# A hybrid decoder trunk on one core: next x transposed as float32r from copied pieces, two chunks behind its gate

## The chip, the cores and the metric

The kernel runs on one core of a Trainium2 chip. The metric is the device time in microseconds, the median of 3 runs. Before the change it is 1412.37 us (1411.79 to 1412.73).

The engines have these names in the profile: PE (matmul; PEld is its weight load), DVE (vector), ACT (scalar), POOL and SP (which here mostly issue DMAs).

## What is computed

Two decoder layers over 512 tokens of 1024 numbers. Each layer mixes tokens, adds the result to its input and normalizes it, runs a squared-ReLU MLP with a normalization behind it, and ends with a gate:

```python
for i in range(DEPTH):
    mix = ssd_mixer(x, ...) if i % 2 == 0 else hgrn2_mixer(x, ...)
    h = layer_norm(DEEPNORM_ALPHA * x + mix, ln_g[i, 0], ln_b[i, 0])
    h = layer_norm(DEEPNORM_ALPHA * h + sq_relu_mlp(h, mlp_w1[i], mlp_w2[i]), ln_g[i, 1], ln_b[i, 1])
    x = h + jax.nn.sigmoid(h @ ple_w_gate[i]) * (p[i] @ ple_w_proj[i])
```

All inputs and outputs are float32. The change lies where the last line is done for the first layer (the first gate) and its result, the next x, is prepared for the second layer's token mixer (HGRN2).

## The kernel before, in words

**Numbers and tiles.** A float32 matrix product is made from three products of float32r operands: each operand is split into hi, a float32r copy made by ACT (L113), and lo, the rest, made by DVE (L116). mm3 (L119 to L122) issues hi*hi, hi*lo and lo*hi into one PSUM bank. The 512 tokens are four chunks of 128 (index c), the 1024 columns two halves of 512 (index h). acc holds the running x with the tokens on the partitions; the products need x with its columns on the partitions, so x is transposed on PE.

**Places.** b8 is a pool of nine places of 8 KB a partition (L52). The split h (h_s, four places) and the split next x (x_n, L616, four places) live there during the first gate; the ninth is free there and is taken later by s3 of values4 (put, L679). PSUM has eight banks: four for pj, one for pt, two for py, one for pm (L57 to L60).

**The first gate** is the end of mlp_and_gate (L616 to L670). For each half h and each chunk c there are 24 matmuls into a bank pg (L658 to L660), then a sigmoid on ACT (L663), a multiplication with the projected p (L664, DVE) and the addition into acc (L666, DVE). The finished 128x512 piece of next x is then turned: turn(h, c) (L620 to L630) transposes it from acc with four PE transposes of 128x128 in float32 against the identity (ident, a part of the constants) into the one bank pt (L625), and three operations read pt one after another: ACT casts it to x_n.hi (L628), ACT copies it to rows (L629), DVE makes x_n.lo (L630). The turn of a chunk isn't issued at once but appended to a list, late, and issued behind the next chunk's gate (L667 to L669). So when the gate ends, one turn is left over.

**values4** (L672 to L729) is the first work of the second layer: the value and gate projections of its first heads, as seven products of 24 matmuls. PE's order is the program's order there (tc.manual_schedule, L1008). Behind the first product stand the left-over turns; then come the others:

```python
        product(part(0, 0), [unit(v) for v in w[0][0]], x, True, first(0, 0))
        for f in late:
            f()
        product(part(0, 1), [unit(v) for v in w[1][0]], z, True, more(0, 0))
```

The first product reads columns of half 0 and tokens of chunks 0 and 1; the second half 1 of the same tokens; the third s3, a difference of two blocks of rows, made at L708 and split at L681 and L682. The later products need the other blocks of rows and the weight sums that DVE makes from weights loaded by POOL (weight_sums, L322).

**Order.** Outside the parts with a written order the framework's scheduler orders each engine's instructions by priority and readiness and sets the waits; each engine then works through its list in order.

Of the kernel before, what the change touches and what calls it, by code (L numbers as in the profile page):

```python
# [9 lines left out]
F32R = mybir.dt.float32r  # L10
# [5 lines left out]
P = 128  # L16
T = 512
# [27 lines left out]
def trunk(ctx: ExitStack, tc, a):  # L45
    nc = tc.nc
    pool = lambda name, bufs, **kw: ctx.enter_context(tc.tile_pool(name=name, bufs=bufs, **kw))
    cpool = pool("consts", 1)
# [3 lines left out]
    b8 = pool("b8", 9)  # L52
# [11 lines left out]
    def nm(s):  # L64
        uid[0] += 1
        return f"{s}_{uid[0]}"

    def mk(p, shape, tag, dt=F32, **kw):
        return p.tile(list(shape), dt, tag=tag, name=nm(tag), **kw)

    def f32(t):
        return t.bitcast(F32)
# [16 lines left out]
    def tmp(tag, shape, dt=F32):  # L89
        return mk(phase[0], shape, tag, dt, bufs=phase[2].get(tag, 1))  # L90

    def bank(p, tag):
        return mk(p, [P, T], tag)
# [8 lines left out]
    def unit(src, lead=LEAD, after=None):  # L102
        n = src.shape[1]
        with tc.high_priority(offset=lead):
            raw = mk(raws, [P, 1024], "raw")
            nc.sync.dma_start(raw[:, :n], src)
        return split(raw[:, :n], lead, after)
# [29 lines left out]
    def project(src, xs, ps, m=P, tok=slice(0, T)):  # L137

        hi, lo = src
        for k in range(8):  # L140
            c = slice(k * m, (k + 1) * m)
            mm3(ps[:m, tok], hi[:, c], lo[:, c], xs.h(k, tok), xs.l(k, tok), k == 0, k == 7)
# [4 lines left out]
    acc = mk(accp, [P, NCH, D], "acc")  # L147
# [32 lines left out]
    ident, triu, eps = cols["ident"], cols["triu"], cols["eps"]  # L180
    convw = cols["convw"].rearrange("p (i k) -> p i k", k=4)
    convb, dskip, snw, hlb, hnw = (cols[n] for n in ("convb", "dskip", "snw", "hlb", "hnw"))
    dtc = cols["dtc"]
    ones = tmp("cm", [P, P])
    nc.gpsimd.memset(ones, 1.0)
    one = mk(cpool, [P, 1], "one")
    nc.gpsimd.memset(one, 1.0)
    ones_s = mk(cpool, [P, 64], "ones_s")
    nc.gpsimd.memset(ones_s, 1.0 / 512)


# [93 lines left out]
    def norm(i, keep=None):  # L285

        gb = ln_params(i)
        h_s = Split(8)
        sums = mk(sm, [P, NCH, 2], "lnsum") if i else None

        def chunk(c):
            with tc.high_priority(offset=LEAD if c == 3 and i % 2 == 0 else 0 if c > 1 and i == 1 else SOON):
                layer_norm(i, c, gb, sums)

        return h_s, chunk, lambda c: transpose_split(acc[:, c, :], h_s, c, c == 3 and i % 2 == 0, keep), sums
# [262 lines left out]
    def mlp_and_gate(layer, h_s, last):  # L558

        w1, w2 = a[f"w1_{layer}"], a[f"w2_{layer}"]  # L560
        blocks = {}
        low = turned_last[0]

        def hidden(g):
            names = ("a11", "a12", "a22", "s1", "s2", "s3", "s4")
            blocks[g] = {
                n: tmp("blk", [P, 2, 4, 256], F32R) if n in ("s3", "s4") else mk(b8, [P, 2, 4, 256], "b8", F32R)
                for n in names
            }
            for p in range(2):  # L570
                tiles = [4 * (2 * g + r) + 2 * p + i for r in range(2) for i in range(2)]
                us = []
                if g == p == 0:
                    for m in tiles[:3]:
                        us.append((unit(w1[m]), bank(psj, "pj")))
                        project(us[-1][0], h_s, us[-1][1], tok=slice(0, 256))
                zs = []
                for r in range(2):
                    z = mk(w4, [P, 2, T], "ab"[r])
                    for i in range(2):  # L580
                        if 2 * r + i < len(us):
                            u, ps = us[2 * r + i]
                            project(u, h_s, ps, tok=slice(256, 512))
                        else:
                            ps = bank(psj, "pj")
                            project(unit(w1[tiles[2 * r + i]], after=low if g == 0 and r == 0 else None), h_s, ps)
                        nc.scalar.activation(z[:, i], ps, AF.Relu)
                        if i == 1:
                            nc.scalar.activation(z, z, AF.Square)
                            zs.append(z)  # L590
                            if r == 1:
                                half_blocks(blocks[g], *zs, p)
                        yield

        for g, period in enumerate(PERIODS):
            if g < 4:
                tiles = hidden(g)
            if g > 0:
                if g == 4:
                    kept = tmp("blk", [P, 2, 4, 256]) if last else None  # L600
                    h_s, after, turned, sums = norm(2 * layer + 1, kept)
                    p_s = (mk(w4, [P, 2, T], "a", F32R), mk(w4, [P, 2, T], "b", F32R))
                    praw = mk(raws, [P, 1024], "raw")
                    nc.sync.dma_start(praw, a[f"pT_{layer}"].rearrange("p k t -> p (k t)"))
                    praw = praw.rearrange("p (k t) -> p k t", k=2)
                    nc.scalar.copy(p_s[0], praw)
                    nc.vector.tensor_sub(p_s[1], praw, f32(p_s[0]))
                w = [[[w2[8 * g - 8 + 4 * i + 2 * j + u] for u in range(2)] for j in range(2)] for i in range(2)]
                products = block_product(w, blocks.pop(g - 1), SUMS[g - 1], g == 1, *((after, turned(0), sums) if g == 4 else ()), low=low if g == 1 else None)
            for op in period:  # L610
                next(tiles if op == "T" else products)

        if last:
            return last_gate(a[f"wp_{layer}"], a[f"wg_{layer}"], h_s, p_s, kept, turned)

        x_n = Split(8)  # L616
        rows = [tmp("blk", [P, 2, 4, 256]) for _ in range(2)]
        late = []

        def turn(h, c):  # L620

            sl = slice(c * P, (c + 1) * P)
            pt = bank(pst, "pt")
            for j in range(4):
                nc.tensor.transpose(pt[:, j * P : (j + 1) * P], acc[:, c, h * 512 + j * P : h * 512 + (j + 1) * P], ident)  # L625
            v = pt.rearrange("p (j t) -> p j t", j=4)
            hh = x_n.hi[h][:, :, sl]
            nc.scalar.copy(hh, v)  # L628
            nc.scalar.copy(rows[c // 2][:, h, :, c % 2 * P : (c % 2 + 1) * P], v)  # L629
            nc.vector.tensor_sub(x_n.lo[h][:, :, sl], v, f32(hh))  # L630

        pps = {}

        def proj(c, pu):

            ps = pps[c] = bank(*((psj, "pj") if c > 1 and pps else (psy, "py%d" % (c % 2))))
            sl = slice(c * P, (c + 1) * P)
            for k in range(2):
                ks = slice(k * 512, (k + 1) * 512)
                mm3(ps, p_s[0][:, k, sl], p_s[1][:, k, sl], pu[0][:, ks], pu[1][:, ks], k == 0, k == 1)  # L640

        for h in range(2):
            pu = unit(a[f"wp_{layer}"][h])
            gu = [unit(a[f"wg_{layer}"][4 * h + j]) for j in range(4)]
            for c in range(NCH):
                sl = slice(c * P, (c + 1) * P)
                if h == c == 0:
                    turns = turned(1)
                    for i in range(NCH):
                        proj(i, pu)  # L650
                        if i in (1, 2):
                            next(turns)
                if h == 1:
                    proj(c, pu)
                turns = turned(c + 2) if h == 0 and c < 2 else None
                pg = bank(psj, "pj")
                sg = tmp("sg", [P, T])
                for k in range(8):  # L658
                    ks = slice((k % 2) * 512, (k % 2 + 1) * 512)
                    mm3(pg, h_s.h(k, sl), h_s.l(k, sl), gu[k // 2][0][:, ks], gu[k // 2][1][:, ks], k == 0, k == 7)  # L660
                    if turns and k in (2, 5):
                        next(turns)
                nc.scalar.activation(sg, pg, AF.Sigmoid)  # L663
                nc.vector.tensor_mul(sg, pps.pop(c), sg)  # L664
                d = acc[:, c, h * 512 : (h + 1) * 512]
                nc.vector.tensor_add(d, sg, d)  # L666
                while late:  # L667
                    late.pop(0)()
                late.append(lambda h=h, c=c: turn(h, c))  # L669
        return x_n, rows, late  # L670

    def values4(xs, rows, late):  # L672
# [333 lines left out]
    x_s, rows, late = mlp_and_gate(0, h_s, False)  # L1006
# [457 lines left out]
```

## Time and profile before

| What | Value |
|---|---|
| median of 3 runs | 1412.37 us |
| span of the profiled execution | 1409.6 us |
| PE busy | 1404.3 us, 100% of the span, 8001 matmuls |
| DVE busy | 1069.1 us, 76% |
| ACT busy | 763.6 us, 54% |
| POOL busy | 45.8 us, 3% |
| first gate to its last matmul | about 705 to 760 us from the span's start |
| values4 on PE | from about 760 us |

The profiled execution's own time is its span of 1409.6 us with what lies around it; no separate time is given for it, and 2.8 us lie between the span and the median of the runs. Lines of the timeline give the start in us from the span's beginning, the length in us, engine, line, operation, and out<-in by the program's names; b is a place of b8 (or of a pool for weights and results), pt the transposes' bank, r a loaded weight block, blk a block of rows. In [...] stands the idle time of the engine before the instruction, and what ended it. The recorded lengths of PE's instructions overlap, since they are pipelined: what an instruction costs is read from the distance of the starts, or from the chain of waits.

### The profile page before, as it was taken

The page shows a single profiled execution, that of the slowest core. Times are in us where ns is not written, and L with a number is a line of the kernel's source. Part 1 is how long each engine was busy: PE and PEld are TensorE (multiplying, and loading weights), DVE is VectorE, ACT ScalarE, POOL GpSimd, SP SyncE. Part 2 cuts the span into 40 slices and gives each one's busy share as a digit, 9 for nine tenths or more (in the row PEclk, how much of TensorE's full clock was granted, in tenths as well). Part 3 has the DMA queues.
Part 4 walks back from the last instruction along what each step waited for, and adds up shares of the span by engine and source line. Part 5 has one row for each costly group of instructions (what it writes and reads, how often), then busy time and mean ns, then how long its engine had stood idle before and what let it go on. Part 6 is the DMA issues. An engine that isn't in the chain of part 4 may idle for free.

```text
span 1409.6 us, 20400 instructions
## 1 busy us (share of the span) xinstructions
PE 1404.3 (100%) x8001; PEld 1168.1 (83%) x8001; DVE 1069.1 (76%) x1778; ACT 763.6 (54%) x1156; POOL 45.8 (3%) x92
## 2 busy tenths in 40 slices
PE   9999999999999999999999999999999999999998
PEld 7888888888988888888888888888898888888887
DVE  7989688698977668677986577678785867667795
ACT  7766465573354444545555547655555454544573
POOL 0000000001000000000000000000100000000100
PEclk9999999999999999999999999999999999999999
DMA  8433333234433444345621421222443444444731
GB/s 313 135 117 120 106 120 110 85 100 156 141 113 127 157 131 152 129 142 178 209 90 49 134 91 61 76 87 96 150 135 105 147 137 148 144 137 159 202 106 60
DMA packets 50399, 181.69 MB, mean 129 GB/s; under 512 B 5632, under 2 KB 6400, under 8 KB 50176
## 3 DMA queue, kind: packets, MB, share of 16 engines
q1 hardware_dynamic: 38784, 138.45, 29.6%
q0 software_dynamic: 11520, 41.95, 9.2%
q8 instruction: 63, 1.03, 0.3%
q14 instruction: 32, 0.26, 0.1%
HBM read 177.16 MB, written 2.16 MB: 127 GB/s over the span
## 4 chain that ended last, share of the span: by engine, by line
PE 99%; DMA 0%; DVE 0%; issue 0%; DVEq 0%
PE pj L120 25%; PE pj L121 25%; PE pj L122 25%; PE py L120 5%; PE py L122 5%; PE py L121 5%; PE py L906 1%; PE pt L238 1%; PE py L1175 1%; PE pm L923 1%; PE pm L871 1%; PE py L1301 1%; PE pt L859 0%; PE py L1303 0%; PE py L1240 0%; PE py L832 0%
## 5 line engine op out<-in xcount | busy, mean ns | idle before, releaser
L113 ACT CAST whi<-raw 128x1024 fp32r<-128x1024 f32 x218 | 228.8, 1050 | 333.2 <-PE pj L121 243.6
L120 PE MATMUL pj<-b,whi 128*128 128x512 f32 (+1 forms) x990 | 378.6, 383 | 0.0
L122 PE MATMUL pj<-b,wlo 128*128 128x512 f32 (+1 forms) x990 | 376.8, 381 | 0.0
L121 PE MATMUL pj<-b,whi 128*128 128x512 f32 (+1 forms) x990 | 376.6, 381 | 0.0
L116 DVE TENSOR_TENSOR wlo<-raw,whi 128x1024 fp32r<-128x1024 f32 x218 | 265.4, 1221 | 129.4 <-ACT whi L113 128.2
L121 PEld LDWEIGHTS pj<-b,whi 128*128 128x128 f32 x990 | 186.4, 188 | 34.6 <-issue 0.9
L122 PEld LDWEIGHTS pj<-b,wlo 128*128 128x128 f32 x990 | 186.3, 188 | 34.5
L120 PEld LDWEIGHTS pj<-b,whi 128*128 128x128 f32 x990 | 186.1, 188 | 34.0
L122 PE MATMUL pj<-whi,b 128*128 128x512 f32 x520 | 204.1, 392 | 0.0
L120 PE MATMUL pj<-whi,b 128*128 128x512 f32 x508 | 202.1, 398 | 0.0
L121 PE MATMUL pj<-wlo,b 128*128 128x512 f32 x508 | 199.2, 392 | 0.0
L113 ACT CAST whi<-r 128x1024 fp32r<-128x1024 f32 x76 | 80.0, 1053 | 68.5 <-PE pj L122 39.4
L122 PEld LDWEIGHTS pj<-whi,b 128*128 128x128 f32 x520 | 97.7, 188 | 20.1
L120 PEld LDWEIGHTS pj<-whi,b 128*128 128x128 f32 x508 | 95.5, 188 | 19.1 <-ACT b L1322 0.3
L121 PEld LDWEIGHTS pj<-wlo,b 128*128 128x128 f32 x508 | 95.5, 188 | 18.7 <-issue 0.2
L116 DVE TENSOR_TENSOR wlo<-r,whi 128x1024 fp32r<-128x1024 f32 x76 | 92.5, 1220 | 19.6 <-ACT whi L113 19.1
L122 PE MATMUL py<-whi,b 128*128 128x512 f32 x260 | 101.3, 390 | 0.0
L121 PE MATMUL py<-wlo,b 128*128 128x512 f32 x248 | 96.6, 389 | 0.0
L120 PE MATMUL py<-whi,b 128*128 128x512 f32 x248 | 96.4, 390 | 0.0
L329 POOL DMA_DIRECT2D r<-in_w x64 | 34.0, 532 | 1098.8 <-DVE wlo L116 544.3
L122 PEld LDWEIGHTS py<-whi,b 128*128 128x128 f32 x260 | 48.8, 188 | 10.2
L800 DVE SCALAR_TENSOR_TENSOR cv<-pj,cst,cv 128x509 f32<-128x509 f32 (+2 forms) x66 | 48.9, 746 | 10.6 <-ACT cv L797 9.8
(368 smaller groups left out, 1943.5 us busy)
## 6 DMA issues: line engine op xcount, KB each, us to landing
raw<-in_w SPq DMA_DIRECT2D x112, 512.0 KB, 3.3
r<-in_w POOLq DMA_DIRECT2D x64, 512.0 KB, 3.8
raw<-in_wssd SPq DMA_DIRECT2D x36, 512.0 KB, 3.9
a<-csd SPq DMA_DIRECT2D x16, 512.0 KB, 4.1
raw<-in_wso SPq DMA_DIRECT2D x16, 512.0 KB, 3.3
raw<-in_whq SPq DMA_DIRECT2D x16, 512.0 KB, 3.4
raw<-in_wg SPq DMA_DIRECT2D x15, 512.0 KB, 4.0
raw<-in_whvg SPq DMA_DIRECT2D x14, 512.0 KB, 3.4
```

Of the source, the lines that this page charges most:

```text
L113: nc.scalar.copy(hi[:, :n], f)
L116: nc.vector.tensor_sub(lo[:, :n], f, f32(hi[:, :n]))
L120: nc.tensor.matmul(out, sh, mh, start=start, stop=False, **kw)
L121: nc.tensor.matmul(out, sh, ml, start=False, stop=False, **kw)
L122: return nc.tensor.matmul(out, sl, mh, start=False, stop=stop, **kw)
L238: nc.tensor.transpose(pt[:, j * P : (j + 1) * P], src[:, k * P : (k + 1) * P], ident)
L329: queue.dma_start(t[i][u], src)
L800: nc.vector.scalar_tensor_tensor(cv[:, d:], ps[:, : T - d], convw[:, i, k : k + 1], cv[:, d:], ALU.mult, ALU.add)
L871: nc.tensor.matmul(pst_[:, c * P : (c + 1) * P], btok[:, c, :], xw[:, c].rearrange("p h q -> p (h q)"), start=True, stop=True)
L906: mm = nc.tensor.matmul(yds[0][64 * r : 64 * r + 64, sl], xdt[:, 2 * c + r, :], m[:, r, sl], start=True, stop=True)
L923: mm = nc.tensor.matmul(yo[:, c * P : (c + 1) * P], pv[:, c - 1].rearrange("p h q -> p (h q)"), cm[:, c * P : (c + 1) * P], start=True, st ...
L1175: nc.tensor.matmul(pcs[r][bs, at : at + n], kk[r][:, ts], qs, start=True, stop=True)
```

## The change

The pieces of next x are no longer transposed from acc. As soon as a piece has been added, POOL issues a DMA that copies its 256 KB, bits unchanged, from acc into pieces[:, c], one of four places of 128x512 in float32r; both halves use the same four. pieces as a whole is one place of b8. The identity is copied once into a float32r tile, eye, by POOL. The four transposes of a turn read the piece and eye in float32r, and write pt seen as float32r. A turn is issued when more than one is in the list, so two chunks behind its own gate, and two are left over at the gate's end. ones_s, the constants of an earlier reduction, moves from the constants' pool to the first phase's pool.

```diff
+    def identity(t):
+        nc.gpsimd.tensor_copy(t, ident)
+        return t
+
+    def same_bits(t, src):
+        nc.gpsimd.dma_start(f32(t), src)
+        return t
+
...
-    ones_s = mk(cpool, [P, 64], "ones_s")
+    ones_s = tmp("ones_s", [P, 64])
...
+        eye = identity(tmp("eye", [P, P], F32R))
+        pieces = mk(b8, [P, 4, T], "b8", F32R)
+
-        def turn(h, c):
+        def turn(h, c, piece):
...
-                nc.tensor.transpose(pt[:, j * P : (j + 1) * P], acc[:, c, h * 512 + j * P : h * 512 + (j + 1) * P], ident)
+                nc.tensor.transpose(pt[:, j * P : (j + 1) * P].bitcast(F32R), piece[:, j * P : (j + 1) * P], eye)
...
-                while late:
+                if len(late) > 1:
                     late.pop(0)()
-                late.append(lambda h=h, c=c: turn(h, c))
+                late.append(lambda h=h, c=c, piece=same_bits(pieces[:, c], d): turn(h, c, piece))
```

## The prediction

> **What bounds the kernel now.** I read the page first, then the chain of waits around the edited place, then the timelines of PE, ACT and DVE there, and last the DMA rows. Of the page three lines matter: span, engines, and the chain by engine.
>
> ```profile
> span 1409.6 us, 20400 instructions
> ...
> PE 1404.3 (100%) x8001; PEld 1168.1 (83%) x8001; DVE 1069.1 (76%) x1778; ACT 763.6 (54%) x1156; POOL 45.8 (3%) x92
> ...
> PE 99%; DMA 0%; DVE 0%; issue 0%; DVEq 0%
> ```
>
> PE ends the kernel: 99% of the chain is PE. So a change counts by the PE time it removes, and by each moment in which PE, which takes its instructions in order, waits. The median is 1412.37 us, 2.8 us over the span; I carry that distance along unchanged. What this kernel's measurement can tell from no change is about 0.2%, 2.8 us.
>
> The chain of waits near the end of the first gate shows what a turn costs PE. Columns: start, length, what.
>
> ```profile
> 759.67 0.23 PE pj L122
> 759.90 0.44 PE pt L625 x4
> 760.34 0.23 PE py L120
> ...
> 765.76 0.23 PE py L122
> 765.99 0.44 PE pt L625 x4
> 766.43 0.23 PE pj L120
> ```
>
> A 128x512 matmul takes PE 0.23 us; the four transposes of one turn take 0.44, 0.11 each. The row of the line in the answer on L625 gives their number:
>
> ```profile
> L625 PE MATMUL pt<-cst,acc x32: 270/272/273, 721.5 to 766.2; 128*128 128x128 f32 x32
> ```
>
> 32 transposes are 8 turns, 3.5 us of PE in all. This is all that the change can win on PE, 0.25%.
>
> **Part 1: the pace of a transpose.** The transposes read float32r in place of float32: the data is the weight load, the identity is streamed. No float32r operation of 128 columns exists before. The nearest rows are the float32r matmuls of 256 columns (chain of waits, first projection of the MLP) beside those of 512 above:
>
> ```profile
> 381.91 0.12 PE pj L120
> 382.03 0.12 PE pj L121
> 382.15 0.12 PE pj L122
> ```
>
> 256 columns take 0.12 us and 512 take 0.23, so 0.11 us per 256 columns and 0.01 fixed; 128 columns streamed alone would be 0.065 us (an estimate from these two rows). That is the lower end, 0.26 us a turn. The upper end without a loss is the pace of now, 0.11, if not the stream but the load of the 128 columns of weights sets it. The rows of the groups by line (last two numbers before the bar's end: busy, mean ns) say how the loads scale:
>
> ```profile
> L121 PEld LDWEIGHTS pj<-wlo,b 128*128 128x128 f32 x508 | 95.5, 188 | 18.7 <-issue 0.2
> ...
> L906 PEld LDWEIGHTS py<-b,xdt 128*64 128x64 f32 x256 | 14.0, 137 | 1.7 <-issue 0.4 <-DVE pv L881 0.4
> ...
> L625 PEld LDWEIGHTS pt<-cst,acc 128*128 128x128 f32 x32 | 4.0, 140 | 1.0
> ...
> L1240 PEld LDWEIGHTS py<-xs,cv 128*32 128x32 f32 x192 | 3.8, 109 | 1.4 <-issue 1.1 <-DVE acc L1094 0.4
> ```
>
> Loads of matmuls with 32, 64 and 128 columns take 109, 137 and 188 ns: about 0.83 ns a column and 82 fixed, so 106 ns in which a load of 128 columns fills its port. But the load of a float32 transpose takes only 140, so 58 above the fixed part: in a transpose the load is faster than that, and the 0.11 us of now is then the float32 stream. I take 0.065, because this row is the nearest one to what is done after; the price is 8 x (0.44 - 0.26) = 1.4 us won. Ends for the range: 0, and 1.8 (128 columns with nothing fixed, 0.055 each, 0.22 a turn). A loss is not excluded either; it is priced as a rival.
>
> The Trainium skill, TensorE: Matmul & The Clock Gate, section on LDWEIGHTS, speaks against this: a load takes about its columns divided by 1.2 GHz, 107 ns for 128. By that rule this part would win nothing; the loads of matmuls here agree (106 ns), the load of the transposes (58) does not.
>
> **Part 2: the copies.** Eight DMAs of 256 KB go through POOL. Their issue (0.5 us each) is free: POOL has nothing to do between its last load and a memset.
>
> ```profile
> 675.03 0.53 POOL L329 DMA_DIRECT2D r<-in_whvg  x1 [1.20 <-DVE wlo L116]
> ...
> 782.25 0.99 POOL L1022 MEMSET sc<- 128x512 f32 x2 [106.69 <-DVE b L682]
> ```
>
> So the copies pass no other transfer on POOL's queue, and what stands behind a copy that waits for its addition is the next copy, and at last that memset, long after. The copy of the identity on POOL and the other home of ones_s are outside every wait of this stage: nothing. A copy must land before its turn. The nearest rows among the DMA issues (last number: us to landing):
>
> ```profile
> r<-in_whvg POOLq DMA_DIRECT2D x8, 512.0 KB, 3.8
> ...
> out<-acc SPq DMA_DIRECT2D x7, 256.0 KB, 2.0
> ...
> r<-r POOLq DMA_DIRECT2D x2, 512.0 KB, 5.6
> ```
>
> Bounds 2.0 (same size, other queue) and 5.6 (same kind and queue, twice the size). I take 4.7, between the two POOL rows. A gate chunk is 24 matmuls, 5.5 us, so with two chunks between addition and turn, seven of the eight land in time even at 5.6. The cover is the gate's matmuls. The eighth has no second chunk behind it.
>
> **Part 3: the turn two chunks later.** Now at the end of the gate one turn is left over and done in values4 behind its first product. After the change two are left over, (1,2) and (1,3), and values4 issues them one behind the other, in PE's order written out there, ahead of the second product. Both need the bank pt, of which there is one. So the second one's transposes wait until the first one's bank has been read three times: cast and copy on ACT, subtraction on DVE. All PE's later work stands behind this wait. The timeline of a turn with nothing in its way, and of the left-over turn of now, with what surrounds it:
>
> ```profile
> 721.47 0.60 PE L625 MATMUL pt<-cst,acc 128*128 128x128 f32 x4
> ...
> 722.10 0.59 ACT L628 CAST b<-pt 128x512 fp32r<-128x512 f32 x1 [1.94 <-PE pt L625]
> ...
> 722.59 0.59 ACT L629 COPY blk<-pt 128x512 f32<-128x512 f32 x1
> ...
> 723.21 0.69 DVE L630 TENSOR_TENSOR b<-pt,b 128x512 fp32r<-128x512 f32 x1 [0.52 <-ACT blk L629]
> ```
>
> ```profile
> 763.42 0.69 DVE L666 TENSOR_TENSOR acc<-sg,acc 128x512 f32<-128x512 f32 x1
> ...
> 765.83 0.60 PE L625 MATMUL pt<-cst,acc 128*128 128x128 f32 x4
> ...
> 766.51 1.05 ACT L113 CAST whi<-r 128x1024 fp32r<-128x1024 f32 x1
> ...
> 767.46 0.59 ACT L628 CAST b<-pt 128x512 fp32r<-128x512 f32 x1
> ...
> 767.94 0.60 ACT L629 COPY blk<-pt 128x512 f32<-128x512 f32 x1
> ...
> 768.74 0.69 DVE L630 TENSOR_TENSOR b<-pt,b 128x512 fp32r<-128x512 f32 x1
> ```
>
> Undisturbed, pt is free 2.4 us after the first transpose (721.47 to 723.90); with one cast ahead on ACT 3.6 us (765.83 to 769.43). On the clock of before, the bank comes free at 768.3 to 769.4. The copy of (1,3) starts behind the addition that ends at 764.11 and lands at 768.8 (bounds 766.1 and 769.7). Without a wait PE would go on at 765.83 + 0.26 = 766.09. The later of bank and copy is about 769.1: PE waits 3.0 us. Ends: 2.2 (bank at 768.3, copy earlier) and 3.6 (copy at 769.7).
>
> **Part 4: the ninth place.** pieces takes the last b8 place, which s3 of values4 has now, in the middle of the gate:
>
> ```profile
> 746.80 1.07 ACT L681 CAST b<-blk 128x1024 fp32r<-128x1024 f32 x1
> ...
> 747.93 1.22 DVE L682 TENSOR_TENSOR b<-blk,b 128x1024 fp32r<-128x1024 f32 x1
> ```
>
> After, s3 waits for a place of h_s, free after the gate's last matmul (759.90). These 1.07 and 1.22 us move into a fuller stretch:
>
> ```profile
> 760.00:770.00 10.00, 10.00 (x49) 8.05 (x47) 7.80 (x11) 6.64 (x10) 0.00 (x0) 1.00 0.31 111
> 770.00:780.00 10.00, 10.00 (x46) 8.29 (x45) 9.97 (x11) 9.07 (x11) 0.00 (x0) 1.00 0.00 0
> ```
>
> From 760 to 770 DVE is idle 2.2 us of 10 and ACT 3.4, and the third product, which reads s3, starts 24 matmuls after 766.43, at 771.9. So it is free, also since the wait of part 3 gives both engines 3 us more before DVE's full stretch (9.97 of 10). If that cover is gone, it is up to 1.2 us ahead of the addition at 763.42, which is in the rival on the copy.
>
> **Sum.** 1409.6 - 1.4 + 3.0 = 1411.2 us of span, 1414.0 with the 2.8 around it: 0.1% longer, within what counts as no change.
>
> **Rivals.**
> *Slower, loads set the pace.* A float32r load in a transpose fills its port for 106 ns as in the matmuls, and the pace stays 0.11. For: the 188 ns rows; against: the 140. Part 1 is then 0 and 3.0 are lost: 1415.4. It decides as soon as the pace is above 0.10; with the wait at 2.8 or more it is over the 0.2%.
> *The last copy is late.* s3's pair stands ahead of the addition (1.2) and the landing takes 5.6: 764.11 + 1.2 + 5.6 = 770.9, a wait of 4.8: 1415.8. For: the r<-r row; against: half the size, and DVE idle at 764.3 to 765.8.
> *No wait.* The two turns get apart, or the bank does not serialize them, and the copy lands in 2 us: 1411.0. For: nothing but the 2.0 us row; against: one bank pt.
> *Narrow float32r in several passes.* The float32 products of L923 show twice as many instructions (x96) as the program's 48 products. If a float32r transpose is split alike, it costs 0.22: 8 x 0.44 = 3.5 us more and 3.0 of wait: 1418.9.
>
> ```profile
> L923 PE MATMUL pm<-cm,pv 128*128 128x128 f32 x96 | 13.4, 276 | 0.0
> ```
>
> **How the numbers follow.** The forecast has 0.53, loads 0.20, late copy 0.10, no wait 0.12, passes 0.05. The range 1410.9 to 1416.2 takes in no wait and late copy with their unsure ends, and leaves out the passes and long waits. Faster by over 0.2% needs 2.8 us, and no case gives it: 0.03. Slower by over 0.2%: half of the loads, two thirds of the late copy, the passes, and a tail of the forecast where the wait is above 4.2: 0.26. The rest, 0.71, is within.
>
> **What would show it.** Right: in the chain, x4 groups of the turns at 0.26 us; one hole of 2 to 4 us on PE right behind the first product of values4, ended by the bank (DVE L630) or, close to it, by the copy; the copies' issues between 716 and 765; s3's pair after 760. Wrong: groups still at 0.44, or longer; no hole; a second hole before the third or fourth product, which would mean that s3 or the next pairs came late (part 4).

## The result, and the profile after

| | before | after |
|---|---|---|
| median of 5 runs | 1412.37 us (1411.59 to 1413.23) | 1417.57 us (1416.79 to 1418.78) |
| ratio after/before | | 1.0038, 95% interval 1.0027 to 1.0049 |
| span of the profiled execution | 1409.6 us | 1415.9 us |

The change makes the kernel 0.38% slower: 5.2 us where 1.6 were forecast, and above the range, which ended at 1416.2. The page of after, the lines that answer to those shown of before (span, engines, chain by engine):

```profile
span 1415.9 us, 20436 instructions
...
PE 1406.8 (99%) x8001; PEld 1169.2 (83%) x8001; DVE 1068.4 (75%) x1778; ACT 763.2 (54%) x1156; POOL 50.4 (4%) x101
...
PE 98%; DVE 1%; ACT 0%; DMA 0%; issue 0%; ACTq 0%; DVEq 0%
```

PE has the same 8001 matmuls and yet is busy 2.5 us longer, and the chain now has a piece that isn't PE. Three places show where. The first is the predicted hole, in PE's timeline at the start of values4:

```profile
765.73 0.40 PE L122 MATMUL py<-whi,b 128*128 128x512 f32 x1
765.97 0.45 PE L636 MATMUL pt<-eye,b 128*128 128x128 f32 x4
769.61 0.54 PE L636 MATMUL pt<-eye,b 128*128 128x128 f32 x4 [3.19 <-DVE b L641]
769.99 0.46 PE L120 MATMUL pj<-whi,b 128*128 128x512 f32 x1
...
770.52 0.58 PE L122 MATMUL pj<-whi,b 128*128 128x512 f32 x1
770.90 0.63 PE L120 MATMUL pj<-whi,b 128*128 128x512 f32 x1
771.33 0.63 PE L121 MATMUL pj<-wlo,b 128*128 128x512 f32 x1
...
774.39 0.39 PE L120 MATMUL pj<-whi,b 128*128 128x512 f32 x1
```

The second left-over turn starts 3.64 us behind the first, of which an undisturbed turn takes 0.29 (starts at 724.73 and 725.02): a wait of 3.35, ended by the third reader of pt (L641 is the old L630). The lines below the hole show the second place. From 770.90 on the starts of the matmuls lie 0.42 to 0.43 us apart where 0.23 is usual, and from 770.52 to 774.39 are ten matmuls in 3.87 us in place of 2.3, so 1.6 us more. The windows of after show the clock there (stretch and length, busy times of PE, PEld, DVE, ACT and POOL, then the granted clock, DMA share and GB/s):

```profile
766.50:769.50 3.00, 0.00 (x0) 0.00 (x0) 2.43 (x3) 2.17 (x4) 0.00 (x0) 1.00 0.49 184
769.50:770.50 1.00, 0.89 (x6) 0.83 (x7) 0.06 (x1) 0.32 (x1) 0.00 (x0) 1.00 0.06 16
770.50:774.00 3.50, 3.50 (x10) 2.71 (x9) 1.82 (x2) 0.76 (x2) 0.00 (x0) 0.51 0.00 0
774.00:778.00 4.00, 4.00 (x19) 3.30 (x18) 3.38 (x4) 2.03 (x3) 0.00 (x0) 1.00 0.00 0
```

Behind the idle stretch the granted clock is at half for some 3.4 us, then full again. PE counts as busy there, so the busy share hides this loss: it is part of the 2.5 us by which PE's busy time grew.

The third place is ahead of the hole. The timeline of PE, first of before and then of after, and that of DVE of after:

```profile
762.71 0.39 PE L122 MATMUL py<-whi,b 128*128 128x512 f32 x1
762.96 0.50 PE L120 MATMUL py<-whi,b 128*128 128x512 f32 x1
```

```profile
762.34 0.39 PE L122 MATMUL py<-whi,b 128*128 128x512 f32 x1
763.11 0.50 PE L120 MATMUL py<-whi,b 128*128 128x512 f32 x1 [0.38 <-DVE sg L675]
```

```profile
757.83 1.22 DVE L693 TENSOR_TENSOR b<-blk,b 128x1024 fp32r<-128x1024 f32 x1
758.97 1.22 DVE L116 TENSOR_TENSOR wlo<-raw,whi 128x1024 fp32r<-128x1024 f32 x1
760.10 2.35 DVE L116 TENSOR_TENSOR wlo<-r,whi 128x1024 fp32r<-128x1024 f32 x2
762.37 0.68 DVE L675 TENSOR_TENSOR sg<-py,sg 128x512 f32<-128x512 f32 x1
```

The first product of values4 needs a bank py that the gate's last multiplication (L675) still reads, and DVE comes to it only at 762.37, behind s3's subtraction (L693) and weight work, one behind the other. PE starts 0.77 us after the matmul ahead, in before 0.25: 0.5 us lost.

What the turns won is read in the chain of waits of after:

```profile
724.66 0.23 PE pj L122
724.89 0.30 PE pt L636 x4
725.19 0.31 PE pj L120
725.49 0.23 PE pj L121
```

A turn takes 0.30 us in place of 0.44, but the matmul behind it 0.31 in place of 0.23: 0.61 against 0.67. By the distances of the starts the pair takes 0.29 + 0.30 in place of 0.35 + 0.32, so 0.60 against 0.67. Eight turns win some 0.6 us.

The sum: 3.35 + 1.6 + 0.5 - 0.6 = 4.85. If the starts of the same matmuls are compared in the two traces from 719 us to behind the clock's fall, after is 4.85 us longer there. The other 0.35 of the 5.2 lie outside this stretch, in unchanged parts (experiment 9 shows how much these move from trace to trace).

### The profile page after: what moved, and what is told of

Its sections match the earlier page's. It is cut to its first block, busy times and chain, and to the rows that moved or that the text cites. A ratio compares the mean times of both kernels' runs of the same rounds, so it can differ in the third digit from the quotient of the medians.

```text
span 1415.9 us, 20436 instructions
## 1 busy us (share of the span) xinstructions
PE 1406.8 (99%) x8001; PEld 1169.2 (83%) x8001; DVE 1068.4 (75%) x1778; ACT 763.2 (54%) x1156; POOL 50.4 (4%) x101
## 4 chain that ended last, share of the span: by engine, by line
PE 98%; DVE 1%; ACT 0%; DMA 0%; issue 0%; ACTq 0%; DVEq 0%
PE pj L120 25%; PE pj L121 25%; PE pj L122 25%; PE py L120 5%; PE py L121 5%; PE py L122 5%; PE py L917 1%; PE pt L246 1%; PE py L1186 1%; PE pm L934 1%; PE pm L882 1%; PE py L1312 1%; PE pt L870 0%; DVE wlo L116 0%; PE py L1314 0%; PE py L1251 0%
```

## Experiments

The ratios are to runs of the kernel before on the same chip (median 1412.24 or 1412.23 there). "Stretch" is, as above, the shift against the first trace of before, from 719 us to behind the first products of values4.

**1. Lateness alone.** The kernel before, float32 from acc and no copies; only the turn comes two chunks later:

```diff
-                while late:
+                if len(late) > 1:
```

> The kernel before with one edit: turns are issued two chunks behind their gate, float32 from acc as before, no copies, no float32r. Theory (the wait for the one bank pt between the two left-over turns, and the half clock that follows an idle PE): PE waits about 3.2 us behind the first product of values4, the granted clock falls in the 4 us after it and costs 1.7 more, so 1412.4 + 4.9 = 1417.3 us. Rival (the copies cost the time, by landing late or by the transfers): nothing of it is here, 1412.4 us.

Measured: 1416.62 us (1415.94 to 1417.86), ratio 1.0030 (1.0019 to 1.0042); stretch +4.95. Its PE timeline and windows:

```profile
765.99 0.60 PE L625 MATMUL pt<-cst,acc 128*128 128x128 f32 x4
769.64 0.66 PE L625 MATMUL pt<-cst,acc 128*128 128x128 f32 x4 [3.05 <-DVE b L630]
```

```profile
766.60:769.60 3.00, 0.00 (x0) 0.00 (x0) 2.42 (x3) 2.10 (x4) 0.00 (x0) 1.00 0.15 61
770.30:773.70 3.40, 3.40 (x9) 2.65 (x9) 1.82 (x2) 1.07 (x2) 0.00 (x0) 0.50 0.00 0
```

The hole and the fall of the clock are there without any copy and without float32r. The change in the order of the turns carries the loss; copies and float32r together add under 1 us to the median and nothing to the stretch. s3's subtraction comes at 756.73 here (747.93 in before), although the ninth place is free. The late turns alone move it: it reads rows that a turn writes, and the difference that makes it (L708) comes at 747.95 in place of 740.64, one chunk later. And no wait for py is listed, though DVE comes to the gate's last multiplication at 762.40, as late as in after: the matmuls shift by 0.15 us there, in after by 0.52.

**2. The two turns apart.** The changed kernel, with the second left-over turn behind the second product:

```diff
-        for f in late:
-            f()
+        late[0]()
         product(part(0, 1), [unit(v) for v in w[1][0]], z, True, more(0, 0))
+        late[1]()
```

> The changed kernel with one edit: of the two left-over turns the second is issued behind the second product of values4, 5.5 us after the first. Theory: no wait for the bank, no fall of the clock; what stays is the gain of the transposes (8 turns x 0.07 = 0.6 us) and a wait of 0.45 us in the first product for a bank that DVE reads late: 1412.2 us. Rival (the copies): they are all still there, and so is their price; about 1417 us, or, if only the landing of the last one counts, as the theory.

Measured: 1420.06 us (1418.04 to 1420.47), ratio 1.0051 (1.0038 to 1.0063); stretch +6.9. A miss. Its PE timeline and a window:

```profile
779.04 0.50 PE L120 MATMUL py<-whi,b 128*128 128x512 f32 x1 [1.05 <-ACT b L692]
...
782.50 0.79 PE L122 MATMUL py<-whi,b 128*128 128x512 f32 x1 [2.72 <-DVE b L693]
```

```profile
781.40:788.10 6.70, 5.60 (x13) 4.45 (x14) 3.31 (x3) 1.50 (x2) 1.28 (x4) 0.50 0.00 0
```

The bank no longer stops PE, but a later product needs the rows of that turn, split by ACT and DVE (L692, L693), and now these come late: 3.8 us of waits in place of 3.2, and the clock at half for 6.8 us (781.35 to 788.17) in place of 3.4. The hole isn't only a matter of the bank: one turn more behind the gate has to be through all its readers before values4 can go on.

**3. Filling the hole.** The changed kernel with twelve matmuls between the two turns, extra work whose result nobody uses:

```diff
-        for f in late:
-            f()
+        late[0]()
+        ps = bank(psm, "pm")
+        for _ in range(12):
+            nc.tensor.matmul(ps, xs.h(0, slice(0, P)), xs.h(1), start=True, stop=True)
+        late[1]()
```

> The changed kernel with 12 matmuls of 128x512 float32r into a spare bank between the two left-over turns, their result unused: 2.8 us of PE work in a wait of 3.3 us. Theory (the clock falls since PE is idle): the wait is as long, but the granted clock stays at 1.00 behind it, and the time is 1.7 us under the changed kernel's: 1415.9 us. Rival (the slow matmuls behind the wait have another cause, such as what ACT, DVE or the transfers do then): they stay slow, 1417.6 us or more.

Measured: 1416.14 us (1415.33 to 1417.51), ratio 1.0026 (1.0016 to 1.0037), with twelve matmuls more than the changed kernel. PE's timeline and a window:

```profile
767.11 0.46 PE L636 MATMUL pt<-eye,b 128*128 128x128 f32 x4
767.40 3.00 PE L725 MATMUL pm<-b 128*128 128x512 f32 x12
770.76 0.46 PE L636 MATMUL pt<-eye,b 128*128 128x128 f32 x3 [0.36 <-DVE b L641]
```

```profile
770.50:774.00 3.50, 3.24 (x17) 2.75 (x18) 1.76 (x3) 1.07 (x2) 0.00 (x0) 1.00 0.00 0
```

The second turn comes 3.65 us behind the first, as before, so the wait costs the same, but the clock stays whole. The stretch is +3.25, 1.6 shorter than in the changed kernel. This separates the two costs: the fall of the clock is a term of its own.

**4. A filler of four.** The same with `range(4)`, again extra work without use.

> The changed kernel with 4 filler matmuls (0.9 us of PE work) between the left-over turns, ahead of the wait, so that 2.3 us of idle time stay. Theory: the wait ends when it did, and the clock stays at 1.00, as after the 2.4 us of the kernel with two banks; values4 is then 1.6 us shorter than in the changed kernel. Rival (any idle time of over 2 us brings the clock down): the clock falls and nothing is won.

Measured: 1416.63 us (one time), stretch +3.25. Two windows of it:

```profile
768.30:770.60 2.30, 0.14 (x1) 0.00 (x0) 1.83 (x2) 1.39 (x3) 0.00 (x0) 1.00 0.27 109
770.60:774.00 3.40, 3.37 (x17) 2.86 (x18) 1.69 (x2) 1.07 (x2) 0.00 (x0) 1.00 0.02 5
```

The 2.2 us of idleness that are left here leave the clock whole.

**5. Two banks.** The changed kernel; the turn (1,3) takes the bank pm:

```diff
-        def turn(h, c, piece):
+        def turn(h, c, piece, p=pst, tag="pt"):
...
-            pt = bank(pst, "pt")
+            pt = bank(p, tag)
...
-                late.append(lambda h=h, c=c, piece=same_bits(pieces[:, c], d): turn(h, c, piece))
+                late.append(lambda h=h, c=c, piece=same_bits(pieces[:, c], d): turn(h, c, piece, *((psm, "pm") if h and c == 3 else ())))
```

> The changed kernel with one edit: turn (1,3) uses the bank pm instead of pt. Theory: the wait for the bank is gone, and the landing of the last copy (2.7 us after PE is there in the changed kernel) ends the wait instead: 0.7 us less, 1416.9 us, if the clock still falls after 2.6 us of idle; 1415.2 us if it needs more idle time than that. Rival (the bank is the whole cause, and the copy lands in time): 1412.5 us.

Measured: 1415.99 us (1415.24 to 1417.87), ratio 1.0028 (1.0017 to 1.0038), stretch +2.45. PE's timeline and a window:

```profile
766.09 0.45 PE L636 MATMUL pt<-eye,b 128*128 128x128 f32 x4
768.95 0.54 PE L636 MATMUL pm<-eye,b 128*128 128x128 f32 x4 [2.41 <-DMA b<-acc]
```

```profile
770.80:774.20 3.40, 3.40 (x17) 2.82 (x16) 3.38 (x4) 0.50 (x1) 0.00 (x0) 1.00 0.00 0
```

With the bank out of the way the last copy ends the wait: the second turn starts 2.86 us behind the first in place of 3.64, so the bank's excess over the copy is only 0.8 us. Two waits lie on top of each other there, as the prediction had it. The same kernel was traced once more:

> The changed kernel with turn (1,3) in the bank pm, once more, for a second trace. Theory: 2.4 us of idle PE are near the point from which the clock falls, so it may fall in this trace or not; if it falls, for 3.4 us, with 1.7 us more than in the first trace. Rival (2.4 us are always too short): the same as the first trace.

It took 1417.12 us (one time), stretch +4.28. Its wait and a window:

```profile
PE pm L636 <- DMA b<-acc: 2.6, 1, 2.6
```

```profile
770.30:773.70 3.40, 3.40 (x10) 2.60 (x8) 1.82 (x2) 0.76 (x2) 0.00 (x0) 0.51 0.00 0
```

This time the clock fell, after 2.6 us of idleness. The same program can pay the 1.6 us or not, and its median lies between the two times that were expected with and without the fall.

The traces show in what the two differ. In all thirteen, every change of the granted clock lies a whole number of periods of 3.413 us behind the trace's first clock record: in after this record, to full, is at 5.96 us and the change to half at 770.55, 764.59 us or 224 periods later, and in experiment 2 from 6.52 to 781.35 are 227. So the stretches to look at are these periods. Here are the two that the wait touches in the first trace, and the last one before the fall in the second:

```profile
763.98:767.40 3.42, 2.56 (x14) 1.95 (x12) 1.81 (x3) 2.16 (x3) 0.54 (x1) 1.00 0.54 169
767.40:770.81 3.41, 1.86 (x11) 1.61 (x12) 2.01 (x3) 2.46 (x5) 0.00 (x0) 1.00 0.16 66
```

```profile
766.93:770.34 3.41, 0.94 (x7) 0.86 (x8) 2.40 (x3) 2.44 (x5) 0.00 (x0) 1.00 0.40 149
```

In the first trace the border of two periods cuts the wait, into 0.9 and 1.55 us; in the second 2.47 us of it lie in one period. Experiment 4 has 0.8 and 1.4 us. No run here sets where the border falls; that it decides rests on all thirteen traces agreeing.

**6. One chunk behind, with copies.** The changed kernel with `while late:` again, so that a piece has one chunk to land:

> The changed kernel with turns one chunk behind their gate, as before the change: copies and float32r stay, one turn is left over, so no two turns want the bank. Theory: the last copy lands at about 768.9 us on the changed kernel's clock and PE is at the turn at 766.0, so PE waits 2.7 us there, and about 0.8 at turn (0,3), whose copy takes 4.6 us; with 0.5 us won by the transposes 1415.3 us, and 1417.0 if the clock falls after the wait. Rival (one chunk covers every copy, the bank is the whole cause): 1412.0 us.

Measured: 1418.28 us (1415.95 to 1420.12), ratio 1.0043 (1.0030 to 1.0055), stretch +7.3. PE's timeline and a window:

```profile
771.42 0.72 PE L636 MATMUL pt<-eye,b 128*128 128x128 f32 x4 [3.03 <-DMA b<-acc]
```

```profile
770.40:777.20 6.80, 5.78 (x17) 4.65 (x18) 2.65 (x3) 1.07 (x2) 0.00 (x0) 0.50 0.01 5
```

Only one turn is left over, and now its copy alone opens a hole of 3.0 us, since only values4's first product covers it; the clock falls for two periods. It falls at 770.41, while PE still waits; the period up to there has 2.0 us of idleness:

```profile
767.00:770.41 3.41, 1.40 (x7) 0.82 (x5) 1.64 (x2) 2.58 (x3) 0.54 (x1) 1.00 0.71 221
```

Another 1.3 us go in a wait for the copy of (0,3), 5.0 us from issue to landing, which one chunk does not cover. Two of the five runs, 1415.95 and 1416.63 us, have a mean granted clock of 1.000, where one period at half would leave 0.999; the others, 1418.28 to 1420.12 us, have 0.998 or 0.999. So the median is a matter of how many runs paid the fall. A copy at the gate's end costs a hole with either order. s3's subtraction is at 760.10 here, so the taken place moves it too.

**7. No copy for the last piece.** As in 6, but (1,3) is transposed in float32 from acc:

```diff
+                if piece is None:
+                    nc.tensor.transpose(to, acc[:, c, h * 512 : (h + 1) * 512][:, js], ident)
...
+                piece = None if h and c == 3 else same_bits(pieces[:, c], d)
```

> As the one before (turns one chunk behind), and the last turn alone, (1,3), is transposed in float32 from acc, without a copy. Theory: no wait in values4; 7 turns win 0.07 us each, the copy of (0,3) costs up to 0.8: 1411.8 to 1412.7 us. Rival (the copies or the ninth b8 place cost time in another way): still above 1414 us.

Measured: 1414.01 us (1413.29 to 1417.11), ratio 1.0014 (1.0005 to 1.0023), stretch +0.97. The waits of PE in this stretch (total, times, longest):

```profile
PE pt L640 <- DMA b<-acc: 0.7, 1, 0.7
PE py L120 <- DVE sg L679: 0.4, 1, 0.4
```

No hole, no fall of the clock, and 3.6 us of the 5.2 are gone. Seven float32r turns still don't beat before: the copy of (0,3) comes 0.7 us late, and the wait for py is there again.

**8. Two chunks behind, last piece from acc in a bank of its own.** As in 7, but with `if len(late) > 1:` and pm for (1,3).

> The changed kernel with its turns two chunks behind, but the second left-over turn, (1,3), is transposed in float32 from acc into the bank pm: neither the bank nor a copy can hold PE there. Theory: both waits and the fall of the clock are gone, what is left is the gain of 0.5 us and the wait of 0.5 us in the first product: 1412.3 us. Rival (two turns at once overload ACT and DVE, whose later work for s2 then holds PE at the fourth product): a wait moves to the fourth product, 1414 us or more.

Measured: 1413.85 us (1413.02 to 1414.38), ratio 1.0013 (1.0004 to 1.0022), stretch +0.66. Its waits:

```profile
PE py L122 <- DVE b L698: 0.4, 1, 0.4
PE py L120 <- DVE sg L679: 0.4, 1, 0.4
```

Above the 1412.3 that was expected. The hole is gone, two small waits take the turns' win back, and about 1 us of the 1.6 over before isn't in this stretch. In this trace the rest lies far from the change: 0.5 us ahead of 690 us, 0.3 near 702 and 0.8 near 1347, where the unchanged kernel's second trace (experiment 9) has 0.3, 0.8 and 0.3 over its first. What sets these places, and whether they are the 1 us of the median, stays open.

**9. Both kernels traced again.** The kernel before, unchanged:

> The kernel before once more, unchanged, for a second trace. Theory: the start of the program, a wait near 702 us and a place near 1347 us differ by up to 1 us from trace to trace in one and the same kernel, so they are no part of the change; the stretch from 719 us to the end of the gate and values4 is the same as in the first trace within 0.1 us. Rival: these places are as in the first trace of before, and the change makes them worse from afar.

1412.72 us (one time), span 1411.0; from 719 us to the end of values4 it agrees with the first trace within 0.05 us. The difference of 1.4 us between the two spans lies elsewhere, for one in a wait that the first trace doesn't have:

```profile
702.59 0.50 PE L120 MATMUL py<-whi,a 128*128 128x512 f32 x1 [0.53 <-DVE lnsum L373]
```

So the sum of the stretch is sharp, and that of the whole span is not, to about 1 us. The changed kernel, unchanged:

> The changed kernel once more, unchanged, for a second trace. Theory: the wait between the left-over turns is again 3.2 us, and the granted clock falls again behind it, for 3.4 us or a multiple of it; 4.7 us between the gate's end and the third product. Rival (the fall needs a special run): the clock stays at 1.00.

1416.99 us (one time), stretch +4.82. The wait was 3.2 us again, and the clock fell again:

```profile
769.90:773.10 3.20, 3.20 (x9) 2.55 (x9) 1.82 (x2) 1.07 (x2) 0.00 (x0) 0.50 0.00 0
```

## Why the prediction was wrong

The prediction's mechanism held: one hole on PE between the two left-over turns, ended by the bank with the copy close by. The sum around it did not.

**The hole (part 3) costs 5.0 us, not 3.0.** The wait itself is 3.35, inside its ends: with a weight's cast ahead of the turn's on ACT (766.65) the bank took the longer of its two times, 3.6 us (765.97 to 769.55), and the copy had landed 0.7 us earlier. The sum took the end of the wait for the end of the loss. The 3.4 us at half clock behind it, worth 1.6 us, are in no term, no rival and no end of the range. Experiment 3 shows that they are a term of their own: filled with work, the same distance between the turns costs 1.6 us less. The page of before could not warn, since PE never idles there long enough and the clock's row shows 9 in all slices, but a forecast that puts 3 us of idleness into a kernel whose PE is busy to 100% has to ask what PE does afterwards. The Trainium skill, TensorE: Matmul & The Clock Gate, Part 1, names this: an idle window of about 3.4 us (3413 ns, free-running) takes PE to half clock. The traces agree on the half, on the length (3.4 us, or 6.8) and on the free-running period (experiment 5); they differ on how idle it must be: a period with 2.0 us of idleness was enough (experiment 6), and 1.55 were not (experiment 5).

**The win (part 1) was mis-sized: 1.4 predicted, 0.6 measured.** The group does run faster: in the chain 0.30 us, where 0.44 was before and 0.26 predicted. The pace that was taken, 0.065 a transpose, holds for half a turn: in the turn at 759.44 the starts of the four and of the matmul behind them lie 0.06, 0.07, 0.08 and 0.08 us apart, where 0.11 lay between the transposes before. And the turn was costed by its own row alone. The matmul behind it was left at 0.23 us, and the chain gives it 0.31. By the starts it took 0.32 before and takes 0.30 now, so how the loss is split between the two hangs on the view; the 0.07 us that the pair wins does not. That loads which the slow transposes covered are what shows now is argued, not shown; the row of the transposes' loads in after still has a mean of 140 ns, so the loads did not get faster with the stream. The rule on LDWEIGHTS of the Trainium skill, TensorE: Matmul & The Clock Gate, that the prediction weighed (a load of 128 columns takes 107 ns, so no win) was nearer to the 0.07 us a turn than the 0.18 taken, but the 0.08 us between the later transposes is below its 107 ns.

**The copies (part 2) held.** POOL's issue cost nothing. The rows of after: the landing of the eight (the median), and the last issue.

```profile
b<-acc POOLq DMA_DIRECT2D x8, 256.0 KB, 2.3
```

```profile
764.90 0.54 POOL L189 DMA_DIRECT2D b<-acc  x1 [9.24 <-PE py L122]
```

Six land in 2.2 to 2.3 us, the fourth in 4.6. The last, issued at 764.90, landed at 768.88, 4.0 us later and 4.6 us behind the end of the addition (764.25), from which the prediction counted its 4.7. None of the first seven made PE wait, as two chunks of cover promised; with one chunk the fourth was 1.3 and 0.7 us late (experiments 6 and 7).

**s3's move (part 4) was said to be free and cost 0.5 us.** The step looked at DVE's idle share from 760 to 770 and had s3 wait for the gate's last matmul. Its cast and subtraction came at 756.73 and 757.83 instead, ahead of that stretch and of that matmul (759.21), so the mark of s3's pair after 760 failed; the late turns alone move it (experiment 1), as does the taken place (experiment 6). DVE reaches the gate's last multiplication at 762.37 with no gap before it, and PE, 0.9 us further on than in before (one turn fewer until there, 0.44, and six turns faster, 0.46), meets the bank that it reads. In experiment 1, with s3 moved as well but slow turns, the shift there is only 0.15 us, so it takes the faster turns to run into it, and most of their win is lost there. No run has faster turns with s3 in its old place, so the share of s3's move in the 0.5 us is argued, not shown.

**The sum.** 1412.4 - 1.4 + 3.0 = 1414.0 was the forecast. With the measured terms it is 1412.4 - 0.6 + 3.35 + 1.6 + 0.5 = 1417.25, and 1417.57 was measured. Of the rivals, none came true as written: the loads' rival had the right sign for part 1 (nearer to nothing than to 1.4), and its time, 1415.4, lacks only the clock and the wait for py. The marks given for a wrong forecast, groups at 0.44, no hole, a second hole, did not appear either; what was wrong lay between the marks.

## What to carry to other kernels

In a PE-bound kernel an idle stretch costs its length and, as soon as about 2 us of it lie in one period of the clock, half of the following 3.4 us: price both, take several traces, since the borders of the periods fall elsewhere in each, and look at the granted clock behind each hole, since the busy share hides it. Cost a faster instruction together with the one behind it, not by its own row. Before work is put off to "later", follow it to the end of the stage: a queue of two left-over pieces with one buffer turns the cover it was meant to win into a wait, and a second buffer, or another place for the turn, here moved the wait to the next that needed it (experiments 5 and 2).

## What the hardware showed that was not expected

The granted clock falls to half for one period of 3.413 us, or two (6.8 us in experiments 2 and 6), always at the border of two periods that run on unbroken from the trace's first clock record, 3.6 to 6.6 us from the span's start. In the traces it fell behind each period with 2.0 to 3.0 us of PE idleness, six times in values4, and behind none there with 1.55 us or less. The idleness need not be one piece: in experiment 2 the clock fell at 781.35, 1.6 us into the second wait, and the first wait's 1.05 us lie in the same period. Where the wait reached into the next period, by 1.15 us (experiment 2) and 1.0 (experiment 6), the clock stayed at half for one more. So the same stretch of 2.4 to 2.6 us costs 1.6 us more or not by where the border falls (experiment 5); where between 1.55 and 2.0 us the limit lies was not measured.
